# Empty instructions at the start of VectorE's and ScalarE's programs in a layer norm with GELU

## The chip, the cores and the metric

One core of a Trainium2 chip. The metric is the device time of one execution in microseconds (us); the median of several executions is quoted. "Span" is the profiled part of one execution, some 2 us shorter than its time.

## The reference

```python
x: 8 x 1024 x 2048 float32; gamma, beta: 2048
mean = np.mean(x, axis=-1, keepdims=True)
var = np.var(x, axis=-1, keepdims=True)
normalized = (x - mean) / np.sqrt(var + eps)
out = gamma * normalized + beta
return 0.5 * out * (1 + np.tanh(np.sqrt(2 / np.pi) * (out + 0.044715 * out ** 3)))
```

67 MB are read and 67 MB are written, at least.

## The kernel before

x is cut into 16 groups of 4 MB; a group is 4 "rows" (tiles of 128 x 2048). There are 5 buffers of 4 MB, `xts`; the result overwrites the input in its buffer, and a buffer is loaded again when its store has landed. Each engine runs a program of its own; they meet at semaphores. Per row, VectorE takes the statistics (4 `bn_stats`, one `bn_aggr`, two small ones) and multiplies by gamma; ScalarE normalizes and later takes the GELU; TensorE adds beta in PSUM; GpSimd takes the power -0.5.

```python
@block.sync                      # loads
def _(sy):
    for b in range(B):
        s = slot(b)
        if stored(b):
            sy.wait_ge(s_store[s], stored(b))      # the buffer's store has landed
        ...                                        # cut: four loads of 1 MB for group 0
        if b:
            sy.dma_start(out=xts[s], in_=xg[b]).then_inc(s_load[s], 16)

@block.vector
def _(ve):
    ...                                            # cut: mean, step and scale, one row's work
    ve.memset(b_hl, 0.0).then_inc(s_m, 1)
    for q in range(R):
        step(slot(0), q, (s_first[q], 16), 2 * q, q - 1 if q else None, q, q)
        if q == 0:
            ve.tensor_tensor(out=split(b_hl[32:33]), ..., op=ALU.subtract)._wait_ge(s_c, 2).then_inc(s_m, 1)
            ve.wait_ge(s_c, 3)                     # gamma is spread over the partitions
    ...                                            # cut: three semaphore resets
    with ve.Fori(0, (B - 1) // SLOTS):             # 3 turns of 20 rows
        ...

@block.scalar
def _(ac):
    ac.preload_act_table(ACT.Gelu_apprx_tanh)
    for k, (p, src) in enumerate(((64, gamma), (0, beta), (32, beta))):
        ac.dma_start(out=row(p), in_=...).then_inc(s_par[k], 16)
    ac.wait_ge(s_m, 1)
    ac.activation(out=split(b_hl[0:1]), in_=row(0), ...)._wait_ge(s_par[1], 16).then_inc(s_c, 1)
    ...                                            # cut: two more copies, then 64 rows, unrolled
```

## Time and profile before

| | before |
|---|---|
| time, median of the first 3 runs | 319.67 us |
| traffic | 134.27 MB |
| VectorE, ScalarE, TensorE busy | 83%, 80%, 77% of the span |
| DMA in the stretches from 40 to 280 us | share 1.00, 431 to 433 GB/s |
| store of group 0 issued, store of group 1 issued | 36.45 us, 53.15 us |
| load into group 0's buffer issued (that store has landed) | 60.75 us |

The prediction below shows the slices, the stretches and the start of the chain of waits. One more view belongs to the argument: the chain of waits (start, length, what) where it leaves the engines.

```profile
132.76 2.09 ACT yk L201
134.85 1.77 ACT xt L208
136.65 41.68 DMA out_dram<-xt
178.34 24.18 DMA xt<-in_x_dram
```

Up to 136 us the chain goes from engine to engine; then it follows a store that takes 41.68 us to land and the load that waited for its buffer. A reader may take from it that the engines bind for 136 us. The stretches (share 1.00 all along) say otherwise.

### The profile page before, as it was taken

How to read it: one execution, taken by the hardware profiler on the slowest of the kernel's cores; microseconds unless marked ns; L12 is line 12 of the kernel's file. 1: busy time of each engine (PE TensorE's matmuls, PEld its weight loads, DVE VectorE, ACT ScalarE, POOL GpSimd, SP SyncE). 2: the span in 40 equal slices, each digit the busy share in tenths (PEclk: the TensorE clock that was granted, in tenths of full speed). 3: DMA queues.
4: the chain of work that ended last, by engine and by line, in shares of the span. 5: the costliest groups of instructions: out<-in, count | busy, mean ns of one | idle time of the engine just before them, and what ended most of it. 6: DMA issues, size and time to landing. Idle time of an engine off the chain costs nothing.

```text
span 317.8 us, 2075 instructions
## 1 busy us (share of the span) xinstructions
PE 244.3 (77%) x520; PEld 57.1 (18%) x520; DVE 265.0 (83%) x514; ACT 253.9 (80%) x132; POOL 79.0 (25%) x73
## 2 busy tenths in 40 slices
PE   2769988888888898888877868598595895868810
PEld 1211222111212122211111111122121111112100
DVE  3499999999999999999969799696996969879500
ACT  2679999999999999999969779696995969968920
POOL 1033323232323231323213222231312213212000
DMA  7999999999999999999999999999999999999994
GB/s 291 438 462 396 459 396 445 412 454 404 458 400 459 422 437 445 412 450 408 458 417 441 437 421 454 404 458 412 450 433 425 450 408 450 408 458 421 437 404 206
DMA packets 5571, 134.27 MB, mean 423 GB/s; under 512 B 656, under 2 KB 704, under 8 KB 704
## 3 DMA queue, kind: packets, MB, share of 16 engines
q1 hardware_dynamic: 2736, 67.11, 49.4%
q10 hardware_dynamic: 2832, 67.13, 49.1%
q14 instruction: 3, 0.02, 0.0%
HBM read 67.13 MB, written 67.11 MB: 422 GB/s over the span
## 4 chain that ended last, share of the span: by engine, by line
DMA 44%; DVE 27%; ACT 19%; PE 3%; issue 2%; ACTq 1%; DVEq 0%; SPq 0%
DMA out_dram<-xt 27%; DVE sts L148 15%; DMA xt<-in_x_dram 15%; ACT yk L201 12%; DVE zg L164 9%; ACT xt L208 7%; PE ps L226 2%; DMA rows<-in_gamma_dram 2%; DVE mvs L157 2%; DVE nms L141 1%; ACTq L216 1%; DVE ves L158 1%; PE ps L243 1%; ACT g_t L197 1%; ACTq L211 0%
## 5 line engine op out<-in xcount | busy, mean ns | idle before, releaser
L148 DVE BATCH_NORM_STATS2 sts<-xt 128x6 f32<-128x512 f32 x256 | 163.5, 681 | 23.7 <-DMA xt<-in_x_dram 21.7
L201 ACT ACTIVATE yk<-xt,nms,rss 128x2048 bf16<-128x2048 f32 x64 | 134.1, 2095 | 41.7 <-DVE nms L141 41.2
L243 PE MATMUL ps<-zg,ident 128*128 128x512 bf16 x256 | 120.8, 627 | 50.9 <-DVE zg L164 50.9
L132 POOL TENSOR_TENSOR rss<-ves,mhalf 128x1 f32<-128x1 f32 x64 | 78.0, 1219 | 216.5 <-DVE ves L158 157.0
L239 PE MATMUL ps<-b_hl,ones_b 33*128 33x512 bf16 x256 | 120.6, 624 | 2.2 <-PEq L234 2.2
L208 ACT ACTIVATE xt<-ps 128x2048 f32<-128x2048 f32 x64 | 118.8, 1857 | 1.5 <-PE ps L243 1.5
L164 DVE TENSOR_TENSOR zg<-yk,g_t 128x2048 bf16<-128x2048 bf16 x64 | 78.0, 1218 | 5.0 <-ACT yk L201 3.0
L243 PEld LDWEIGHTS ps<-zg,ident 128*128 128x128 bf16 x256 | 27.6, 130 | 144.1 <-DVE zg L164 108.7
L239 PEld LDWEIGHTS ps<-b_hl,ones_b 33*128 33x128 bf16 x256 | 27.0, 127 | 92.1 <-issue 88.4
L157 DVE BATCH_NORM_AGGREGATE mvs<-sts 128x2 f32<-128x24 f32 x64 | 16.9, 264 | 2.2
L141 DVE TENSOR_SCALAR nms<-mvs,rss 128x1 f32<-128x1 f32 x64 | 12.6, 196 | 0.0
L226 PE MATMUL ps<-rows,ones 1*128 1x512 f32 x8 | 7.2, 1072 | 6.0 <-DMA rows<-in_gamma_dram 6.0
L158 DVE TENSOR_SCALAR ves<-mvs 128x1 f32<-128x1 f32 x64 | 9.8, 154 | 2.2
L194 ACT ACTIVATE b_hl<-rows 1x2048 bf16<-1x2048 f32 x1 | 1.9, 1909 | 4.9 <-DMA rows<-in_beta_dram 4.9
L226 PEld LDWEIGHTS ps<-rows,ones 1*128 1x128 f32 x8 | 2.5, 323 | 9.2 <-DMA rows<-in_gamma_dram 6.0
L172 DVE TENSOR_TENSOR b_hl<-rows,b_hl 1x2048 bf16<-1x2048 f32 x1 | 2.3, 2281 | 2.1 <-ACT b_hl L195 2.1
L197 ACT ACTIVATE g_t<-ps 128x2048 bf16<-128x2048 f32 x1 | 1.9, 1877 | 2.4 <-PE ps L226 2.4
L190 ACT ACT_TABLE_LOAD x1 | 1.3, 1283 | 0.9 <-SPq L106 0.9
L167 DVE MEMSET b_hl<- 33x1024 uint32 x1 | 0.9, 912 | 1.2 <-SPq L106 1.2
L195 ACT ACTIVATE b_hl<-rows 1x2048 bf16<-1x2048 f32 x1 | 1.9, 1908 | 0.0
L123 POOL MEMSET ones<- 65x128 f32 x1 | 0.2, 202 | 0.5 <-SPq L106 0.5
L127 POOL TENSOR_SCALAR_AFFINE_SELECT ident<-ident 128x128 bf16<-128x128 bf16 x1 | 0.3, 294 | 0.1
(7 smaller groups left out, 0.9 us busy)
## 6 DMA issues: line engine op xcount, KB each, us to landing
xt<-in_x_dram SPq DMA_DIRECT2D x15, 4096.0 KB, 24.3
out_dram<-xt ACTq DMA_DIRECT2D x15, 4096.0 KB, 37.0
xt<-in_x_dram SPq DMA_DIRECT2D x4, 1024.0 KB, 8.1
out_dram<-xt ACTq DMA_DIRECT2D x4, 1024.0 KB, 12.7
rows<-in_beta_dram ACTq DMA_DIRECT2D x2, 8.0 KB, 5.6
rows<-in_gamma_dram ACTq DMA_DIRECT2D x1, 8.0 KB, 5.0
```

The source lines that it names most:

```text
L132: po.tensor_tensor(out=rss[:, c], in0=ves[:, c], in1=mhalf, op=ALU.pow)._wait_ge(s_a, k + 1).then_inc(s_q, 1)
L141: ve.tensor_scalar(out=nms[:, c], in0=mvs[:, q, 0:1], scalar1=rss[:, c], scalar2=-1.0, op0=ALU.mult, op1=ALU.mult)._wait_ge(s_q, count).th ...
L148: ins = ve.bn_stats(out=sts[:, q, j, :], in_=xr[:, j, :])
L157: ve.bn_aggr(out=mvs[:, q], in_=sts[:, q])._wait_ge(s_o, count + 1).then_inc(s_o, 1)
L158: ve.tensor_scalar(out=ves[:, q:q + 1], in0=mvs[:, q, 1:2], scalar1=float(eps), scalar2=1.0, op0=ALU.add, op1=ALU.mult)._wait_ge(s_o, coun ...
L164: ve.tensor_tensor(out=zgs[q % 2], in0=yks[q % 2], in1=g_t, op=ALU.mult)._wait_ge(s_n, count).then_inc(s_z, 1)
L197: ac.activation(out=g_t, in_=pss[0], func=ACT.Identity)._wait_ge(s_tg, 1).then_inc(s_c, 1)
L201: ac.activation(out=yks[t % 2], in_=xts[slot(b)][:, q], func=ACT.Identity, scale=rss[:, q:q + 1], bias=nms[:, q:q + 1])._wait_ge(s_p, t + ...
L208: ins = ac.activation(out=xt[:, q], in_=pss[i % 2], func=ACT.Gelu_apprx_tanh)._wait_ge(s_t, i + 1)
L226: ins = pe.matmul(pss[0][:, cols(j)], lhsT=ones[64:65], rhs=rows[64:65, j * K // nsub:(j + 1) * K // nsub, :d // K], start=True, stop=True)
L239: ins = pe.matmul(ps[:, cols(j)], lhsT=ones_b, rhs=b_hl[:, cols(j)], start=True, stop=False)
L243: ins = pe.matmul(ps[:, cols(j)], lhsT=ident, rhs=zgs[k % 2][:, cols(j)], start=False, stop=True)
```

## The change

The trace of the kernel before has a DMA queue named `instruction`, with three packets of 8 KB inside the span (34.3, 99.5 and 109.9 us). I take them for fetches of the next part of an engine's program. "Sequencer" stands for what the traces list as `DVEq` and `ACTq` beside the busy work of VectorE and ScalarE: semaphore increments and DMA issues. The intent is to place some 70 instructions that do nothing ahead of the work, so that the border between two parts is crossed while the engine waits for its first load anyway.

```diff
+PAD_DVE, PAD_ACT = 76, 68
...
                 ve.memset(b_hl, 0.0).then_inc(s_m, 1)
+                for _ in range(PAD_DVE):
+                    ve.nop()
                 for q in range(R):
...
                     ac.dma_start(out=row(p), in_=...).then_inc(s_par[k], 16)
+                for _ in range(PAD_ACT):
+                    ac.nop()
                 ac.wait_ge(s_m, 1)
```

## The prediction

> **What bounds the kernel now.** I read the page from the whole to the part: first the busy slices, then a table of busy time by stretches of the span, then the start of the chain of waits, then the waits of VectorE, and last narrow windows of the DMA view, in which the instruction fetches can be dated. The slices first:
>
> ```profile
> DVE  3499999999999999999969799696996969879500
> ACT  2679999999999999999969779696995969968920
> ...
> DMA  7999999999999999999999999999999999999994
> ```
>
> VectorE (DVE) and ScalarE (ACT) are full in the first half and have gaps in the second. The DMA row has no gap between its first and its last slice. That says which resource never rests, but a 9 covers anything from 90% up, so I cut the span into stretches. In each row come the window, its length, the engines with instruction counts, the granted clock, the DMA share and the GB/s:
>
> ```profile
> 40.00:80.00 40.00, 35.51 (x77) 8.27 (x78) 39.15 (x78) 36.95 (x20) 11.33 (x9) 1.00 1.00 431
> 80.00:120.00 40.00, 35.40 (x78) 8.23 (x77) 39.09 (x78) 37.10 (x20) 12.80 (x10) 1.00 1.00 431
> 120.00:160.00 40.00, 35.56 (x79) 8.24 (x78) 38.97 (x78) 36.77 (x20) 10.41 (x9) 1.00 1.00 433
> 160.00:200.00 40.00, 30.58 (x67) 6.87 (x65) 34.04 (x66) 32.14 (x18) 10.88 (x9) 1.00 1.00 433
> ```
>
> The last two numbers are the point: a share of 1.00 and 431 to 433 GB/s, the same while VectorE is full (39.15 of 40) and after it has begun to wait (34.04 of 40). So the speed of VectorE does not set the rate of the transfers. The traffic is fixed: 134.27 MB (67.13 read, 67.11 written). At 432 GB/s that is 311 us. Transfers start about 2 us into the span and run dry near 313.6; then 4.2 us of landing and closing work follow. 2 + 311 + 4 = 317, against a span of 317.8. The kernel is bound by its traffic from one end to the other.
>
> The change acts in the first 16 us, so I read the chain of waits there:
>
> ```profile
> 0.94 5.04 DMA rows<-in_gamma_dram
> ...
> 6.02 7.20 PE ps L226 x8
> ...
> 13.25 1.89 ACT g_t L197
> ...
> 15.16 0.02 DVEq L174
> ...
> 15.23 0.69 DVE sts L148
> ```
>
> The preparation of the parameters is set by the load of gamma and eight slow matmuls on TensorE (to 13.22), then by one ScalarE copy (to 15.13), for which VectorE waits before its second row. Neither VectorE's first row nor ScalarE's first two copies lie on this path. Their waits:
>
> ```profile
> DVE sts L148 <- DMA xt<-in_x_dram: 21.7, 8, 3.7
> ...
> DVE b_hl L172 <- ACT b_hl L195: 2.1, 1, 2.1
> DVE sts L148 <- ACT g_t L197: 2.0, 1, 2.0
> ```
>
> VectorE has 2.1 us and 2.0 us of idle time in the prologue after its first row, besides 3.7 us before it (the longest of the eight load waits). The other seven load waits, 18 us together, all come late and are the sign of a compute side that has caught up with the DMA.
>
> **Where the fetches are now.** The page's DMA queue list shows them as a queue of their own: 3 packets, 0.02 MB, so 8 KB each. By narrow windows I find one in each of 34 to 35, 99 to 100 and 109.5 to 110.5 us, and none in 0 to 34. The first window's row reads:
>
> ```profile
> q14 instruction: 1, 0.01, 2.0%
> ```
>
> 2.0% of 16 engines over 1 us is 0.32 us of one engine. Do they stall anybody? The timeline of VectorE around the first:
>
> ```profile
> 31.72 0.69 DVE L148 BATCH_NORM_STATS2 sts<-xt 128x6 f32<-128x512 f32 x1
> ...
> 35.85 0.69 DVE L148 BATCH_NORM_STATS2 sts<-xt 128x6 f32<-128x512 f32 x1
> ```
>
> The row that contains the fetch takes 4.13 us, the rows before it 4.12 us (23.48, 27.60, 31.72). Around 99 us the starts are 98.51 and 102.64, again 4.13. ScalarE's starts around 109.9 us are 103.70, 107.81 and 111.93, so 4.11 and 4.12. No fetch inside the span costs anything that can be seen. The two at 34 and 99 us lie some 65 us or 16 rows apart; a VectorE row has 8 instructions, and 16 x 8 = 128 instructions of 64 bytes are 8 KB. So I take these two for VectorE's and the one at 110 us for ScalarE's. That is an inference.
>
> [...]
>
> **The change part by part.** Removed: nothing. Added: 76 empty instructions on VectorE, after its first memset and before its first row, and 68 on ScalarE, after its three parameter DMAs and before its first wait. Moved: the point in the program where a fetch falls. The loads of x are issued by SyncE and the parameter loads by ScalarE ahead of its empty instructions, so no transfer starts later.
>
> *Cost of the empty instructions.* No row has one on these engines. VectorE's semaphore instructions at the loop's entry are shown at 0.02 us, but they follow each other at 0.10 us (26.66 to 26.75 in the chain), the dispatch included. I take 0.1 us as the upper estimate and 0.03 us as the lower one (the spacing of back-to-back configuration instructions on GpSimd). VectorE: 76 x 0.03 to 0.1 = 2.3 to 7.6 us, from about 1.2 us, so done at 3.5 to 8.8 us. The first row starts at 5.82 now, so it is late by 0 to 3.0 us. It ends at 8.78 now, and its next piece waits until 10.93 anyway, so 2.1 us of a delay vanish there; the remaining 0.9 us go into the 2.0 us ahead of the second row. ScalarE: 68 x 0.03 to 0.1 = 2.0 to 6.8 us from 2.9 us, done at 4.9 to 9.7 us, against a first copy at 7.05: late by 0 to 2.65 us. Its two copies would end at up to 13.5 instead of 10.89, and the VectorE subtraction (2.28 us) at up to 15.8 instead of 13.2. The second row starts at 15.23 now. Worst case: 0.7 us late there, central case (0.05 us per instruction): 0.
>
> [...]
>
> *Gain.* The fetches at their old places cost 0 to 0.01 us each: 3 x 0.01 = 0.03 us at most. With more instructions ahead, later blocks also cross earlier, so fetches in mid-run will not all disappear.
>
> *Effect of a late row on the end.* The first store is issued at 36.45. The first five groups of loads (20.97 MB at 426 GB/s) keep the DMA busy to about 1.9 + 49 = 51 us even without a store. So a delay of up to 14 us leaves no hole in the DMA. At the end the last store is issued at 305.3 while the DMA runs to 313.6, which is 8.3 us x 420 GB/s = 3.5 MB of backlog for a store of 1.05 MB, some 5.8 us of spare. Sum: 0.0 us on the end, with a worst case of a few tenths through another mixture of reads and writes.
>
> **Rivals.** (1) The compute side is on the path until 136 us: the chain of waits does run through VectorE and ScalarE up to there before it turns to the store. Then a late start of 0.7 to 2.7 us would be passed on: up to 322.4 us. Against it speaks the share of 1.00 in every stretch; a chain shows who released whom, not that the DMA had room. (2) [...] Against it: rows of 4.12 and 4.13 us and three runs within 0.57 us. (3) The new alignment makes VectorE's loop of 160 and more instructions fetch again at each of its turns[...]. (4) The later first store lets loads run alone for longer; the rates differ by little (426 GB/s for loads alone, 432 mixed, 421 for stores alone), so a shift of 2 us is worth about 0.03 us.
>
> **Range and chances.** The main line gives the old time, 319.67, less at most 0.03; I write 319.6. The three runs spread from 319.23 to 319.8, and a different order of loads and stores may add about as much again, so 318.9 to 320.5 should hold it 8 times in 10. Either 2% bound is 6.4 us away; no rival alone reaches it. Chances: faster 0.01, within 2% 0.98, slower 0.01.
>
> **What would show it right or wrong.** The table by stretches should keep a share of 1.00 and 431 to 433 GB/s, with the DMA dry near 313.6. The DMA view of the first 6 us should show instruction packets that were not there, and the windows at 34 and 110 us none. VectorE's first row should start between 5.8 and 9 us, and its second between 15.2 and 16. The load waits of VectorE (21.7 us) may shrink by whatever the start is late. I am wrong if the rows before 136 us change their 4.12 us, if the DMA shows a slice below 9 in mid-run, or if the end moves by more than 1 us while the GB/s stay the same.

The term for the fetch at its new place: with it the worst case came to rows 2.7 us late, without it to 0.7 us; the 2.7 us and the 322.4 us of Rival 1 still contain it. Rival 2: that a fetch at its old place holds an engine up in some executions. The sum on the end stayed at 0.0 us with the term and without, so the forecast of 319.6 us (319.67 less at most 0.03) does not rest on it. The 64 bytes of an instruction agree with the compiled streams of `e1_real_both` below.

## The result, and the profile after

The changed kernel took 319.75 us (median of 6 runs, 319.33 to 319.91), the kernel before 319.69 us (6 runs, 319.23 to 320.06). The ratio is 1.0002, 95% interval 0.9989 to 1.0015. Ratios here are the mean time of one kernel's fast runs over that of the other's in the same rounds, so not quite the ratio of the medians. The predicted 319.6 us and its range held.

The mechanism did not. The head of the changed kernel's page, and its busy instructions on VectorE and ScalarE:

```profile
span 317.9 us, 2075 instructions
...
PE 244.4 (77%) x520; PEld 57.3 (18%) x520; DVE 265.1 (83%) x514; ACT 253.9 (80%) x132; POOL 79.0 (25%) x73
```

2075 instructions: the page of the kernel before has the same count. 144 were added in the source, and none was recorded. The profile does record such instructions where there are any: two `NOP`s of SyncE stand in both traces. So I looked where the fetches are. The list of DMA queues in the window from 0 to 34 us of the changed kernel (packets, MB, share of 16 engines):

```profile
q1 hardware_dynamic: 896, 13.63, 95.5%
q10 hardware_dynamic: 96, 0.02, 0.3%
```

There is no instruction queue in it. In the windows 34 to 35, 99 to 100.2 and 108.5 to 109.5 us it is there, with one packet each, as in the kernel before. (There, the third is at 109.9 us.) No fetch has moved from its place in the program. I then compared the two compiled programs byte for byte: all five instruction streams are identical (VectorE's has 15,232 bytes, ScalarE's 12,992, at 64 bytes an instruction). The empty instructions were dropped somewhere between the source and the compiled program. The two "kernels" are one program, and the comparison above is a measurement of the noise.

The stretches of the changed kernel, in the columns of the prediction, are accordingly those of before:

```profile
40.00:80.00 40.00, 35.51 (x77) 8.26 (x78) 39.16 (x78) 36.95 (x20) 11.32 (x9) 1.00 0.99 429
80.00:120.00 40.00, 35.42 (x78) 8.25 (x77) 39.09 (x78) 37.09 (x20) 12.79 (x10) 1.00 1.01 434
...
160.00:200.00 40.00, 30.81 (x67) 7.02 (x65) 34.07 (x67) 32.17 (x18) 10.72 (x9) 1.00 1.00 433
```

What remains is the question that the change meant to ask: what would the padding be worth if it were there? And is it true that the DMA hides whatever happens at the start?

### The profile page after: what moved, and what is told of

Same layout as the page of the kernel before. It is cut to its first block, busy times and chain, and to the rows that moved or that the text cites. A ratio compares the mean times of both kernels' runs of the same rounds, so it can differ in the third digit from the quotient of the medians.

```text
span 317.9 us, 2075 instructions
## 1 busy us (share of the span) xinstructions
PE 244.4 (77%) x520; PEld 57.3 (18%) x520; DVE 265.1 (83%) x514; ACT 253.9 (80%) x132; POOL 79.0 (25%) x73
## 4 chain that ended last, share of the span: by engine, by line
DMA 44%; DVE 27%; ACT 19%; PE 3%; issue 2%; ACTq 1%; DVEq 0%; SPq 0%
DMA out_dram<-xt 26%; DMA xt<-in_x_dram 16%; DVE sts L149 15%; ACT yk L206 12%; DVE zg L165 9%; ACT xt L213 7%; PE ps L231 2%; DMA rows<-in_gamma_dram 2%; DVE mvs L158 2%; DVE nms L142 1%; ACTq L221 1%; DVE ves L159 1%; PE ps L248 1%; ACT g_t L202 1%; ACTq L216 0%
```

## The experiments

All on the chip, in three groups; the kernel before ran beside each group (medians 319.67, 319.71 and 319.79 us). A base theory (A: traffic binds, the start is hidden) stood against Rival B (compute before 136 us binds, a late start is passed on) and Rival C (the fetches at their old places cost something).

### Padding that is really there

In place of each empty instruction stands an increment of a semaphore for which nobody waits. The compiled streams grow by 4,864 and 4,352 bytes, exactly 76 x 64 and 68 x 64.

```diff
-                    ve.nop()
+                    ve.sem_inc(s_pd, 1)
...
-                    ac.nop()
+                    ac.sem_inc(s_pa, 1)
```

> The empty instructions of the change left no trace on the chip (2075 instructions in both profiles, fetches at the same times), so here 76 and 68 semaphore increments nobody waits for stand in their place. Theory A (the empty ones were never in the program; real ones move the fetch, but the DMA hides it all): VectorE's and ScalarE's sequencers show the increments at about 0.1 us each, two instruction fetches fall before 12 us instead of at 34 and 110 us, VectorE's first row starts at 9 to 11 us instead of 5.8, its second row at 15 to 18 us, the time stays within 0.2% of before (319.1 to 320.3). Rival B (compute before 136 us is on the path, and a late second row is passed on): the time rises by what the second row is late, 0.7 to 2.7 us. Rival C (the fetches at their old places cost something): the time falls by 0.5 us or more.

Measured: 319.77 us, ratio 0.9999 (0.9985 to 1.0012). 2219 instructions, which is 2075 + 144. The increments of VectorE's line in this kernel's trace (engine, operation, count; duration; first and last start), first all of them, then in the windows 5 to 6, 6 to 7 and 7 to 8 us:

```profile
L172 DVEq EVENT_SEMAPHORE  x76: 21/21/21, 1.0 to 8.4; - x76
...
L172 DVEq EVENT_SEMAPHORE  x11: 21/21/21, 5.0 to 5.9; - x11
...
L172 DVEq EVENT_SEMAPHORE  x7: 21/21/21, 6.0 to 7.0; - x7
...
L172 DVEq EVENT_SEMAPHORE  x11: 21/21/21, 7.1 to 8.0; - x11
```

Each lasts 21 ns by its row, but they start 93 ns apart, 11 to a microsecond. In one microsecond there are only 7: at one place the distance is 500 ns. I take that for the border: it holds the sequencer for 500 - 93 = 407 ns. On ScalarE the distance is 72 ns, and at one place 401 ns:

```profile
L199 ACTq EVENT_SEMAPHORE  x12: 17/17/17, 6.0 to 6.8; - x12
...
L199 ACTq EVENT_SEMAPHORE  x12: 17/17/17, 7.2 to 8.0; - x12
```

Now the instruction queue is in the first 34 us, with two packets (at 10.0 and 10.6 us, some 3.5 us after the gaps):

```profile
q1 hardware_dynamic: 895, 13.60, 95.3%
q10 hardware_dynamic: 96, 0.02, 0.3%
q14 instruction: 2, 0.02, 0.1%
```

The increments go on behind the gap while these packets have yet to move, so the sequencers did not wait for them. In every kernel here with real padding, the gap stands behind the 59th increment on VectorE and behind the 56th on ScalarE and has the same length, by the single starts in the traces. So it belongs to a place in the program.

VectorE's first row starts at 8.47 us instead of 5.82 (9 to 11 were expected), and its second row at 15.15 instead of 15.23. The timeline of VectorE shows where the delay vanished (start, length, operation, in brackets the idle time before it):

```profile
8.47 2.47 DVE L151 BATCH_NORM_STATS2 sts<-xt 128x6 f32<-128x512 f32 x4 [6.34 <-issue]
...
12.02 2.28 DVE L177 TENSOR_TENSOR b_hl<-rows,b_hl 1x2048 bf16<-1x2048 f32 x1 [0.59 <-ACT b_hl L202]
15.15 0.70 DVE L151 BATCH_NORM_STATS2 sts<-xt 128x6 f32<-128x512 f32 x1 [0.85 <-ACT g_t L204]
```

The two waits of 2.1 and 2.0 us in the kernel before have shrunk to 0.59 and 0.85. TensorE's chain from gamma still ends last, as before.

The same with one engine's padding alone:

> The real padding on VectorE alone, ScalarE as before. Theory A: the fetch of VectorE at 34 us moves to before 12 us and the one at 99 us to about 60 us, which shows these two to be VectorE's; the one at 110 us stays; time within 0.2% of before. If the fetch at 110 us moves too, my assignment of fetches to engines was wrong. Rival B: up to 1 us longer.

> The real padding on ScalarE alone. Theory A: the fetch at 110 us moves to before 12 us, the ones at 34 and 99 us stay, a new one of ScalarE may come at about 200 to 220 us; ScalarE's first copy starts at 9 to 11 us instead of 7; time within 0.2% of before. Rival B: up to 2.7 us longer.

Measured: 319.76 us, ratio 0.9999 (0.9984 to 1.0015), and 319.62 us, ratio 0.9997 (0.9982 to 1.0013). The fetches, dated by narrow windows:

| kernel | fetches inside the span, us |
|---|---|
| before | 34.3, 99.5, 109.9 |
| changed (empty instructions) | 34.4, 99.8, 108.9 |
| padding on both | 10.0, 10.6, 64.1, 216.7 |
| on VectorE alone | 10.3, 63.8, 109.0 |
| on ScalarE alone | 10.7, 34.3, 100.0, 216.1 |

So the fetches at 34 and 99 us are VectorE's and the one at 110 us is ScalarE's. ScalarE's padding moves its fetch to the start and brings one more at 216 us: with 68 more instructions its program crossed one border more. None of it moves the time. ScalarE's first copy starts at 8.14 us in the kernel with its padding alone, again ahead of the 9 to 11 expected. C has no support in the full kernel: the three intervals leave room for a gain of 0.6 us at most. B cannot be judged here, as the second row was not late.

### A start that is really late

To judge B, something must be late. Chained memsets on a spare tile hold VectorE back ahead of its first row; no padding.

```diff
                 ve.memset(b_hl, 0.0).then_inc(s_m, 1)
+                for i in range(20):                      # 20, 36, 8, 13, 16
+                    ins = ve.memset(idle, 0.0).then_inc(s_pd, 1)
+                    if i:
+                        ins._wait_ge(s_pd, i)
```

> No padding, but 20 chained memsets of about 1 us on VectorE before its first row, so that the whole compute side starts about 12 us late (second row at some 27 us, first store at some 48 us). Theory A: the first loads keep the DMA busy until about 51 us, so there is no hole and the time stays within 0.5% of before (318.1 to 321.3). Rival B (compute is on the path until 136 us): about 12 us longer, 331 to 333.

> 36 memsets in place of 20: second row at some 43 us (28 us late), first store at some 64 us. Theory A: now the loads run dry at about 51 us and the DMA has a hole of some 13 us before the first store, so the time rises by about 13 us, to 329 to 336. Rival B: by the whole 28 us, to some 347.

Both expectations of A missed: 326.30 us (ratio 1.0207, 1.0192 to 1.0223) and 345.46 us (ratio 1.0806). In part the delay was mis-sized: a chained memset takes 1.19 us, not 1, so the first store came at 52.22 us (15.8 us late) and 71.29 us (34.8 us late). But between these two, 19.1 us of more delay cost 19.2 us of more time: past some point every late microsecond is passed on. Three smaller delays were to find that point.

> The 20 memsets cost 1.19 us each and made the first store 15.8 us late, more than the 14 us of slack that I had worked out, and the time rose by 6.6 us; 36 made it 34.8 us late and cost 25.8 us, so beyond the knee each us of delay costs a full us. 8 memsets should make the first store 1.5 us late (8 x 1.19 less 8.1). Theory A: time within 0.2% of before. Rival B (every late us is passed on): 1.5 us longer, 321.2.

> 13 memsets, first store about 7.4 us late. Theory A with my slack of 14 us, and also with a knee at 9.2 us (15.8 less 6.6): time within 0.2% of before. Rival B: 7.4 us longer, 327.

> 16 memsets, first store about 11.0 us late. With my slack of 14 us: time within 0.2% of before. With a knee at 9.2 us, because the DMA loses time already when it is left with a single transfer in flight: about 1.8 us longer, 321.5, and DMA shares below 0.97 somewhere between 50 and 120 us. Rival B: 11 us longer.

| memsets | first store late by, us | second store issued, us | time, us | ratio (95%) |
|---|---|---|---|---|
| 0 | 0 | 53.15 | 319.67 to 319.79 | |
| 8 | 1.5 | 54.62 | 320.02 | 1.0039 (0.9990 to 1.0089) |
| 13 | 7.4 | 60.58 | 321.07 | 1.0048 (1.0032 to 1.0065) |
| 16 | 11.0 | 64.16 | 323.45 | 1.0122 (1.0105 to 1.0139) |
| 20 | 15.8 | 68.93 | 326.30 | 1.0207 (1.0192 to 1.0223) |
| 36 | 34.8 | 88.00 | 345.46 | 1.0806 (1.0786 to 1.0825) |

(The interval of 8 memsets is wide through one run of 323.02 us; the other three lie from 319.88 to 320.11. The second store of 36 memsets starts 16.7 us after the first.) Of the last three expectations, theory A held for 8 memsets only. For 13 it missed, also with the knee at 9.2 us: the time rose by 0.4% and not by less than 0.2%. For 16 that knee promised 1.8 us more, and 3.7 were measured.

B falls for small delays: 7.4 us late cost 1.3 us, not 7.4. My slack of 14 us falls too: at 11.0 us late the time had risen by 3.7 us. The stretches of the kernel with 16 memsets, around 62 us (window, length, PE, PEld, DVE, ACT, POOL, clock, DMA share, GB/s), show the hole:

```profile
60.00:62.00 2.00, 2.00 (x6) 0.56 (x5) 2.00 (x5) 1.73 (x2) 0.00 (x0) 1.00 0.61 262
62.00:63.00 1.00, 1.00 (x3) 0.15 (x1) 0.93 (x4) 1.00 (x2) 0.41 (x1) 1.00 0.00 0
63.00:64.00 1.00, 0.59 (x2) 0.13 (x2) 1.00 (x2) 1.00 (x1) 1.00 (x1) 1.00 0.74 197
```

and its SyncE, its own queue, and ScalarE say why:

```profile
62.91 0.33 SPq L121 DMA_DIRECT2D xt<-in_x_dram  x1
...
64.16 0.34 ACTq L222 DMA_DIRECT2D out_dram<-xt  x1
```

The first five loads are all in by then. The only transfer on the way is the first store; when it has landed, the next load is issued at 62.91 us, and until its data flow nothing moves. The second store, which would have filled the hole, is issued only at 64.16 us. So the second store must be on the way before the first has landed. In the kernel before, it goes out at 53.15 us and the first one lands by 60.75 us, which looks like a room of 7.6 us. But a later start moves that landing too. With 13 memsets the load that waits for it is issued at

```profile
63.62 0.33 SPq L121 DMA_DIRECT2D xt<-in_x_dram  x1
```

which is 3.0 us after the second store (60.58), not 0.2. With 16 it is 1.25 us before the second store. So the hole opens somewhere between 7.4 and 11.0 us of delay, at about 10 by a straight line between the two (an estimate).

The cost is not a single knee either. From 7.4 to 15.8 us late, each more microsecond cost about 0.6 us, by the times above against the kernel before of the same group; from 15.8 to 34.8 us it cost 1.0. The second bend lies where the prediction put the end of the first loads. With 36 memsets their data run dry between 51 and 52 us, and nothing moves until the first store (71.29 us):

```profile
51.00:52.00 1.00, 1.00 (x3) 0.14 (x1) 1.00 (x3) 1.00 (x1) 0.00 (x0) 1.00 0.03 8
...
53.00:71.00 18.00, 14.99 (x33) 3.55 (x34) 17.73 (x35) 15.17 (x9) 7.12 (x5) 1.00 0.00 0
```

With 20 memsets the first store goes out at 52.22 us, just at that end; every microsecond later than this lengthens an empty stretch.

What the 13 memsets lost (1.3 us) is not explained by a hole: from 60 to 120 us the share stayed at 1.00, but the DMA moved 420 GB/s instead of 435, and 60 x 15 / 435 = 2.1 us is more than enough. Why it was slower was not tested. A share of 1.00 alone does not show that no time is lost; the GB/s belong beside it.

### The same with less traffic

Theory A says that the full DMA hides the start. Then less traffic must uncover it. Only the left half of each result row is stored (a wrong result).

```diff
-  ac.dma_start(out=og[b], in_=xt)
+  ac.dma_start(out=og[b, :, :, :d // 2], in_=xt[:, :, :d // 2])
```

> Only the left half of each result row is stored (wrong result on purpose), which takes 33.6 of 134.3 MB from the DMA: 100.7 MB are 233 us at 432 GB/s, less than the 64 rows of VectorE at 4.17 us (267 us). So compute sets the end: some 285 to 297 us, VectorE busy in tenths 9 to the end. It is the base for the next two.

> The same half stores with the 20 memsets of before. With compute as the bound the 12 us of late start must show in full in the end: 11 to 13 us over the half-store kernel. If it does not, the reading that the DMA's fullness is what hides a late start in the full kernel falls.

> The same half stores with the real padding (76 and 68 semaphore increments). With compute as the bound any gain or loss of the padding must show: Theory A (fetches at their old places cost nothing) says 0 to 3 us longer than the half-store kernel, by as much as the second row is late in the trace; Rival C (early fetch removes a stall) says shorter.

Measured: 295.53 us with half stores, 311.42 us with the 20 memsets on top (11 to 13 us more were expected, for a delay taken as 12 us), 295.63 us with the real padding on top. VectorE is full to the end in the half-store kernel, and the DMA is not:

```profile
DVE  3499999999999999999999999999999999999940
...
DMA  7999999999999979799999979899999984070643
```

Here the 20 memsets delay the first store by 52.22 - 36.31 = 15.9 us, and this is passed on whole: 311.42 - 295.53 = 15.9 us. In the full kernel they cost 6.6. So the traffic does hide a part of a late start, and without it nothing is hidden. The padding costs 0.1 us, inside the scatter, with VectorE as the bound (its second row starts at 15.06 us, in the half-store kernel at 15.09), and gains nothing either. Rival C falls here too, within that scatter of some 0.3 us: moving the first fetches from mid-run to the start is worth nothing even where VectorE sets the end.

## Why the prediction was right or wrong

- **The time: right, but by luck as far as this change goes.** The two kernels are one program, so their times had to agree under any theory of the padding. Only the real padding (319.77 us) tested the forecast, and it held.
- **The bound: right.** The stretches stay at a share of 1.00, and taking 25% of the traffic away brought the time down by 24 us until VectorE bound.
- **The gain of at most 0.03 us: not contradicted.** It was read from the rows' even spacing. The real padding shows no gain, but its interval (0.15%, some 0.5 us) cannot resolve 0.03 us.
- **The added cost of the empty instructions: wrong.** The step "76 x 0.03 to 0.1 = 2.3 to 7.6 us" took it for granted that what stands in the source runs on the chip. It was 0 instructions and 0 us. The forecast that fetches would show in the first 6 us, and none at 34 and 110, failed, and this is what gave it away. What the runs showed in its place is one program: 2075 instructions in both profiles and identical compiled streams.
- **The cost had they been real: nearly right**, with increments as the stand-in (an empty instruction that does reach the chip was not run). VectorE's increments took from 1.0 to 8.5 us, near the upper estimate, which was taken from the same kind of instruction. The first row came 2.65 us late (predicted 0 to 3.0 without a stall), and the second not late at all.
- **The fetch at its new place: mis-sized.** My term for it was an estimate that no trace had shown, and too large; the gaps are 0.41 us on VectorE and 0.33 us on ScalarE (401 - 72 ns), and the packets move only after the sequencers have gone on (some 3.5 us after the gaps). So what was paid at a border is not the wait for that packet. If the packets trail the border as far in mid-run, I looked for a stall one row too late; but the rows before (from 27.60 and 94.40 us) take 4.12 us too.
- **Which fetch is whose: right**, by the runs with one engine's padding.
- **The room of 14 us: wrong.** It was reckoned to the end of the first loads (51 us), with the first store as what must come in time. But the first store alone leaves the DMA with one transfer; a first hole comes when that lands, from a delay of between 7.4 and 11.0 us on, and some loss without a hole came at 7.4 us already. The 51 us were right for something else: from there on every microsecond of delay is paid in full. The change never came near either, so the error did not show in the time.
- **Rival 1** (compute on the path until 136 us) is wrong for the first few microseconds (7.4 us late cost 1.3) and right only where the first store comes after the first loads have run dry (15.8 us late and more). The chain of waits named engines that could have been several microseconds later at a cost of a fraction. **Rival 2** has no support: the three kernels with real padding stand at ratios of 0.9997 to 0.9999. **Rival 3** (new fetches at the loop's turns) did not occur: VectorE's real padding moved its two fetches and added none. **Rival 4** was too small by my figures; the 420 GB/s of the 13 memsets suggest, but do not show, that the rate depends somewhat on what is on the way together.

## What to carry to other kernels

Before explaining what an added instruction does, see in the profile or the compiled program that it is there: count the instructions, and find the event that it was meant to move. A border between two parts of a program cost 0.33 to 0.41 us of a sequencer's time here, and nothing that could be seen in mid-run (rows of VectorE of 4.13 us with a fetch, 4.12 without) or where the engine waited anyway (VectorE's second row at 15.15 us with the padding, 15.23 without). How late the start might be was set here first by the moment at which the DMA was left with no second transfer (a share of 0.00 from 62 to 63 us with 16 memsets, 11.0 us late); the end of the first loads, at about 51 us, set only from where on every late microsecond was paid in full (19.1 us more cost 19.2). Some was lost even before any hole (1.3 us at 7.4 us late).
